# A float32 decoder trunk on one core: feature-major products as three matmuls of 256 columns, and new starts for the weight parts in their buffers

## The chip, the cores and the metric

The kernel runs on one core of one Trainium2 chip. The metric is the device time of one execution in microseconds. What follows "before" is the kernel as it was; "after" is the changed one.

## The reference

The reference is a decoder trunk of two layers over 256 tokens with 2048 features, in float32. Each layer normalises, mixes tokens, adds the result to `x`, normalises again, and adds a gated feed-forward part.

```python
for i in range(DEPTH):                       # DEPTH = 2, x is (1, 256, 2048) float32
    h = rms_norm(x, attn_norm[i])
    y = moba_attention(...) if i == 0 else mla_attention(...)
    x = x + y
    h = rms_norm(x, ffn_norm[i])
    x = x + conv_glu_ffn(h, w_gate, w_up, conv_w, conv_b, w_down)

def conv_glu_ffn(h, w_gate, w_up, conv_w, conv_b, w_down):     # 2048 -> 5632 -> 2048
    g = causal_depthwise_conv(h @ w_gate, conv_w, width=3) + conv_b
    return (silu(g) * (h @ w_up)) @ w_down
```

With 256 tokens and blocks of 256 keys, the first layer's block-sparse attention is plain causal attention with 16 heads of 128. The second is latent attention: queries and keys/values go through ranks of 512, with 128 plain and 64 rotary features a head. Nearly all the work is in the products with the weights, some 390 MB of float32, each used once.

## The kernel before

**Two parts of each number.** To keep float32 accuracy the kernel writes every operand as a high part in `float32r`, TensorE's faster float32 form, and a low part, the rest. A product is then high x high + high x low + low x high. An activation tile holds both parts side by side: columns 0 to 255 are the high part of 256 tokens, 256 to 511 the low part. This is so for `h` (the normalised input), `oT` (attention's output) and `a` (the feed-forward's inner activations).

**The stream of weights.** `Stream` carries the weights from memory to TensorE in the order of their use. A unit is one transfer of mostly 1 MB, issued by SyncE into one of three `raw` buffers (line 75). It holds four pieces of 128 x 512. For each piece, ScalarE casts the high part into a buffer `whi` (line 103) and VectorE subtracts it from the weights into `wlo` (line 104). Each of these has five buffers of 512 + 64 elements, and a piece may begin a few elements into its buffer: the function `starts` gives that for each unit and piece. There are 370 units and 1480 pieces.

**Quanta and side work.** The program is written in order by hand. A quantum is TensorE's work on one piece. Beside each quantum stand functions (`at`, `first`) that record the rest at that place: norms, evacuations, attention's steps. The final loop splits up to four pieces ahead, then records the quantum, then its side work.

**Token-major products** (`tok_major`, lines 246 to 248) load 128 tokens of the activation as weights and move a weight piece of 512 columns past them: three matmuls for each half of the tokens. They are the first attention's queries, keys and values (units 0 to 47, four head groups) and the latent layer's up-projections (units 200 to 221).

**Feature-major products** load 128 x 128 of the weight piece and move the activation. There are two forms. `feat_major` (lines 272 and 274) takes, for each of a piece's four blocks, one matmul of 512 columns (the weights' high part against both parts of the activation) and one of 256 (the weights' low part against the high part). Its result is in two halves of a PSUM bank, which `halves` adds: ScalarE copies one half to SBUF (line 293) and VectorE adds (line 297 and, with a residual, 295). Gate and up, down, and the latent layer's `wq_a` use it. `feat_half` (lines 286 to 288) takes three matmuls of 256 columns, all into the same half of a bank, so that nothing is left to add; two outputs share a bank. The output projections (`plan_wo`) and the very last down tile use it.

**Order of stages.** First attention (units 0 to 47), its output projection (48 to 63), gate and up (64 to 151), down (152 to 195), `wq_a` (196 to 199), latent attention (200 to 221), its output projection (222 to 237), gate and up (238 to 325), down (326 to 369). Attention's last heads are still under way while an output projection begins. A norm's column sums (line 361) and the spreading of its result over rows (line 371) are small matmuls between the first quanta of the stage that follows.

**Starts before.** The weight parts of gate, up, down and `wq_a` begin at 0. The others go through steps of 8 elements (32 bytes): `HEAD_STARTS` has one step for each of the twelve groups of four units, the output projections go through steps 0 to 7, two units each, and `LATENT_STARTS` has a step for each unit.

Of the kernel before, what the change touches and what calls it, by code (L numbers as in the profile page):

```python
# [10 lines left out]
F32 = mybir.dt.float32  # L11
# [6 lines left out]
P = 128  # L18
# [25 lines left out]
AHEAD_PIECES = 4  # L44
WO_OPEN = 8

UP_ORDER = ("pairs", "pairs")
DOWN_ORDER = ("pairs", "pairs")

ROOM = 64  # L50

HEAD_STARTS = (2, 1, 3, 2, 1, 3, 4, 5, 6, 7, 0, 2)
LATENT_STARTS = (1, 2, 3, 4, 5, 6, 7, 2, 2, 1, 1, 3, 3)

H_START = 8

# [58 lines left out]
def trunk(ctx: ExitStack, tc: tile.TileContext, a, out):  # L115
# [38 lines left out]
    units += units_of("ffn_down1")  # L154
    def starts(u, j):

        step = 0
        if u < 48:
            step = HEAD_STARTS[u // 4]
        elif u < 64 or 222 <= u < 238:  # L160
            step = (u - 48) // 2 % 8 if u < 64 else (u - 222) // 2
        elif u == 200:
            step = 2
        elif 201 <= u < 209:
            step = u - 201
        elif 209 <= u < 222:
            step = LATENT_STARTS[u - 209]
        return 8 * step, 8 * step

    assert len(units) == 370  # L170
    ws = Stream(nc, raw_pool, part_pool, units, starts)


# [73 lines left out]
            mm(o, hi, t_lo[:, :n], start=False, stop=False)  # L247
            mm(o, lo, t_hi[:, :n], start=False, stop=kt == k_last)  # L248

    def feat_major(state, rhs, k0, k_last, t_hi, t_lo, n, order="pairs"):  # L250

        if k0 == 0:
            state["acc"] = ps_acc.tile([P, 512], F32, name="acc")
        src, o = rhs(), state["acc"]
        ks = range(n // P)
        steps = {
            "pairs": [(k, part) for k in ks for part in "hl"],  # L260
            "low first": [(k, part) for k in ks for part in "lh"],
            "grouped": [(k, part) for part in "hl" for k in ks],
        }[order]
        for i, (k, part) in enumerate(steps):
            kt = k0 + k
            flags = dict(
                start=k0 == 0 and i == 0, stop=kt == k_last and i == len(steps) - 1,
                skip_group_check=True,
            )
            c = slice(k * P, (k + 1) * P)  # L270
            if part == "h":
                mm(o, t_hi[:, c], src[:, kt, :], **flags)  # L272
            else:
                mm(o[:, :S], t_lo[:, c], src[:, kt, :S], **flags)  # L274

    def open_half(state):
        state["acc"] = ps_acc.tile([P, 512], F32, name="acc")

    def feat_half(state, rhs, k0, k_last, first, t_hi, t_lo, n, half):

        src = rhs()
        o = state["acc"][:, half * S : (half + 1) * S]
        for k in range(n // P):
            kt = k0 + k
            w_hi, w_lo = t_hi[:, k * P : (k + 1) * P], t_lo[:, k * P : (k + 1) * P]
            mm(o, w_hi, src[:, kt, :S], start=first and k == 0, stop=False, skip_group_check=True)  # L286
            mm(o, w_hi, src[:, kt, S:], start=False, stop=False, skip_group_check=True)  # L287
            mm(o, w_lo, src[:, kt, :S], start=False, stop=kt == k_last, skip_group_check=True)  # L288

    def halves(dst, acc, base=None):  # L290

        t = small.tile([P, S], F32, name="half", bufs=2)
        nc.scalar.copy(t, acc[:, S:])  # L293
        if base is not None:
            nc.vector.tensor_tensor(t, t, base, op=ALU.add)
        dst = t if dst is None else dst
        nc.vector.tensor_tensor(dst, acc[:, :S], t, op=ALU.add)  # L297
        return dst


    class Norm:
# [77 lines left out]
    def residual(state, j, half):  # L379
        nc.vector.tensor_tensor(  # L380
            xT[:, j, :], xT[:, j, :], state["acc"][:, half * S : (half + 1) * S], op=ALU.add
        )

    def residual_halves(state, j):
        halves(xT[:, j, :], state["acc"], xT[:, j, :])

    def store(j):
        nc.sync.dma_start(out[:, j, :], xT[:, j, :])
# [258 lines left out]
    def plan_wo(norm, order):  # L647

        states = {}
        seen = set()  # L650

        done = {}
        ready = []
        last = None
        for j, kq in order:
            pr = j // 2
            states.setdefault(pr, {})
            fresh = pr not in seen
            seen.add(pr)

            def work(t_hi, t_lo, n, j=j, kq=kq, pr=pr, fresh=fresh):
                if fresh:
                    open_half(states[pr])
                feat_half(states[pr], lambda: env["oT"], 4 * kq, KD - 1, fresh, t_hi, t_lo, n, j % 2)

            last = add(work)
            done[j] = done.get(j, 0) + 1
            if done[j] == 4 and done.get(j ^ 1, 0) == 4:
                for jj in (j & ~1, j | 1):
                    at(last, residual, states[pr], jj, jj % 2)  # L670
                    ready.append((last, jj))
        nxt = 0.0
        for i, (q, jj) in enumerate(ready):
            nxt = max(nxt, q + 1)
            if i < KD - 2:
                norm.plan(int(nxt), jj)
                nxt += 2.5
            else:
                at(int(nxt) - 1, norm.now, jj)
        at(last + 3, norm.sums)  # L680
        at(last + 4, norm.rows)
        return last
# [19 lines left out]
    class FTile:  # L702
# [7 lines left out]

        def evac_gate(self):
            self.g = ffn["g"][self.j % 2]
            halves(self.g[:, 2:], self.gate["acc"])
            nc.vector.tensor_tensor(self.g[:, 2:], self.g[:, 2:], self.norm.rstd_b, op=ALU.mult)

        def conv_last(self):
            self.c = ffn["pool"].tile([P, S], F32, name="c")
# [15 lines left out]
            nc.vector.tensor_tensor(self.c, self.c, self.norm.rstd_b, op=ALU.mult)  # L733

        def product(self):
            u = halves(None, self.up["acc"])
            nc.vector.tensor_tensor(self.c, self.c, u, op=ALU.mult)

        def high(self):
            nc.scalar.copy(ffn["a"][:, self.j, :S], self.c)  # L740
# [7 lines left out]
    def plan_gate_up(layer, norm):  # L748
        for j in range(NF):
            f = FTile(layer, j, norm)  # L750
            for kind, st in (("g", f.gate), ("u", f.up)):
                for kq in range(4):
                    q = add(lambda t_hi, t_lo, n, st=st, kq=kq: feat_major(
                        st, lambda: norm.h, 4 * kq, KD - 1, t_hi, t_lo, n, UP_ORDER[layer]))
                if kind == "g":
                    if j == 0:
                        at(q, open_ffn, layer)
                    at(q, f.evac_gate)
                    at(q + 1, f.conv_last)
                    at(q + 2, f.conv_rest)  # L760
                    at(q + 3, f.silu)
                    at(q + 4, f.scaled)
                else:
                    at(q, f.product)
                    at(q + 1, f.high)
                    at(q + 2, f.low)
# [2 lines left out]

    n3 = Norm(C_AN + KD, False)  # L770

    def plan_down_feat(norm, layer):
        for j in range(KD):
            st = {}
            tail = norm is None and j == KD - 1
            if tail:
                first(len(quanta), open_half, st)
            for kq in range(NF // 4):
                if tail:
                    q = add(lambda t_hi, t_lo, n, st=st, kq=kq: feat_half(  # L780
                        st, lambda: ffn["a"], 4 * kq, NF - 1, kq == 0, t_hi, t_lo, n, 0))
                else:
                    q = add(lambda t_hi, t_lo, n, st=st, kq=kq: feat_major(
                        st, lambda: ffn["a"], 4 * kq, NF - 1, t_hi, t_lo, n, DOWN_ORDER[layer]))
            if tail:
                at(q, residual, st, j, 0)
            else:
                at(q, residual_halves, st, j)
            if norm is None:
                at(q, store, j)  # L790
            elif j < KD - 1:
                norm.plan(q + 2, j)
            else:
                at(q, norm.now, j)
                at(q + 3, norm.sums)
        return q

    plan_down_feat(n3, 0)


    att2 = ExitStack()
# [84 lines left out]

    def cq_part(state, r):
        g = par[:, C_GQA + r : C_GQA + r + 1]
        src = halves(None, state["acc"])
        hi, lo = env["cqT"][:, r, :S], env["cqT"][:, r, S:]  # L890
        nc.scalar.activation(hi, src, AF.Copy, scale=g)
        nc.vector.scalar_tensor_tensor(lo, src, g, hi.bitcast(F32), op0=ALU.mult, op1=ALU.subtract)
        if r == 0:
            cq["acc"] = att_pool.tile([P, S], F32, name="cacc", bufs=1)
            nc.scalar.activation(cq["acc"], src, AF.Square)
        else:
            sq = small.tile([P, S], F32, name="nsq", bufs=3)
            nc.scalar.activation(sq, src, AF.Square)
            nc.vector.tensor_tensor(cq["acc"], cq["acc"], sq, op=ALU.add)
# [17 lines left out]
    for r in range(4):  # L917
        state = {}
        for kq in range(4):
            q = add(lambda t_hi, t_lo, n, st=state, kq=kq: feat_major(  # L920
                st, lambda: n3.h, 4 * kq, KD - 1, t_hi, t_lo, n))
            if r == 0 and kq == 0:
                at(q, open_mla)
        at(q, cq_part, state, r)
# [97 lines left out]
    plan_wo(n4, WO_ORDER2)  # L1022
    plan_gate_up(1, n4)

    plan_down_feat(None, 1)


    assert len(quanta) == len(ws.pieces), (len(quanta), len(ws.pieces))
# [121 lines left out]
```

## Time and profile before

| | |
|---|---|
| median of 3 runs | 2138.59 us (2138.43 to 2138.74) |
| the profiled execution's own time | 2138.94 us |
| its span | 2137.1 us |
| granted TensorE clock | 1.0 |
| PE busy | 2129.4 us (100%), 12439 matmuls |
| weight loads (PEld) | 1883.5 us (88%) |
| VectorE busy | 1461.7 us (68%) |
| ScalarE busy | 1184.6 us (55%) |
| read from memory | 387.01 MB, 182 GB/s over the span |

PE is TensorE's matmuls, PEld its weight loads, DVE VectorE, ACT ScalarE, POOL GpSimd and SP SyncE. L272 is line 272 of the kernel. A row of instructions reads: engine, operation, result <- operands, shapes, number; then, by the view, durations and the first and last start, or busy time, mean duration and idle time before. Matmuls overlap in the pipeline and their ends are modelled, so that durations of one line add up to more than the span. Numbers of a stretch from a table of windows read: from:to and length, then for each engine busy time and number of instructions, then the granted clock, the DMA's busy share and GB/s.

### The profile page before, as it was taken

The page shows a single profiled execution, that of the slowest core. Times are in us where ns is not written, and L with a number is a line of the kernel's source. Part 1 is how long each engine was busy: PE and PEld are TensorE (multiplying, and loading weights), DVE is VectorE, ACT ScalarE, POOL GpSimd, SP SyncE. Part 2 cuts the span into 40 slices and gives each one's busy share as a digit, 9 for nine tenths or more (in the row PEclk, how much of TensorE's full clock was granted, in tenths as well). Part 3 has the DMA queues.
Part 4 walks back from the last instruction along what each step waited for, and adds up shares of the span by engine and source line. Part 5 has one row for each costly group of instructions (what it writes and reads, how often), then busy time and mean ns, then how long its engine had stood idle before and what let it go on. Part 6 is the DMA issues. An engine that isn't in the chain of part 4 may idle for free.

```text
span 2137.1 us, 33882 instructions
## 1 busy us (share of the span) xinstructions
PE 2129.4 (100%) x12439; PEld 1883.5 (88%) x12439; DVE 1461.7 (68%) x3246; ACT 1184.6 (55%) x2418; POOL 45.6 (2%) x37
## 2 busy tenths in 40 slices
PE   9999999999999999999999999999999999999999
PEld 7888889988888888888889889998888888888888
DVE  6766666777777777755556786777777777765554
ACT  6555555555555555545455675555555555554443
POOL 0000000000000000000000110000000000000000
PEclk9999999999999999999999999999999999999999
DMA  7444445455555555555554433555555555555553
GB/s 268 160 175 178 158 158 191 176 186 197 184 191 196 182 194 192 187 195 185 198 188 156 177 132 119 178 178 197 182 193 194 182 196 189 186 202 205 189 203 129
DMA packets 59350, 391.30 MB, mean 183 GB/s; under 512 B 6960, under 2 KB 10032, under 8 KB 13232
## 3 DMA queue, kind: packets, MB, share of 16 engines
q1 hardware_dynamic: 59040, 389.10, 51.6%
q8 instruction: 98, 1.61, 0.3%
q14 instruction: 68, 0.56, 0.1%
q10 hardware_dynamic: 144, 0.04, 0.0%
HBM read 387.01 MB, written 2.10 MB: 182 GB/s over the span
## 4 chain that ended last, share of the span: by engine, by line
PE 97%; DVE 1%; DMA 0%; issue 0%; ACT 0%; POOL 0%; SPq 0%; POOLq 0%; ACTq 0%; DVEq 0%
PE acc L272 45%; PE acc L274 24%; PE acc L247 5%; PE acc L248 5%; PE acc L246 5%; PE acc L286 3%; PE acc L288 3%; PE acc L287 3%; PE sc L511 1%; PE tp L487 1%; PE sc L558 1%; PE tp L547 0%; PE sc L514 0%; DVE wlo L104 0%; PE sc L559 0%; DMA xT<-in_xT 0%
## 5 line engine op out<-in xcount | busy, mean ns | idle before, releaser
L104 DVE TENSOR_TENSOR wlo<-raw,whi 128x512 fp32r<-128x512 f32 (+1 forms) x1480 | 991.1, 683 | 385.9 <-ACT whi L103 382.5
L103 ACT CAST whi<-raw 128x512 fp32r<-128x512 f32 (+1 forms) x1480 | 866.4, 614 | 280.3 <-PE acc L272 173.9
L272 PE MATMUL acc<-h,whi 128*128 128x512 f32 x2880 | 999.2, 390 | 0.0
L274 PE MATMUL acc<-h,wlo 128*128 128x256 f32 x2880 | 812.1, 282 | 0.0
L272 PEld LDWEIGHTS acc<-h,whi 128*128 128x128 f32 x2880 | 540.6, 188 | 113.1
L274 PEld LDWEIGHTS acc<-h,wlo 128*128 128x128 f32 x2880 | 544.3, 189 | 0.0
L272 PE MATMUL acc<-a,whi 128*128 128x512 f32 x1364 | 472.9, 390 | 0.0
L274 PE MATMUL acc<-a,wlo 128*128 128x256 f32 x1364 | 384.6, 282 | 0.0
L272 PEld LDWEIGHTS acc<-a,whi 128*128 128x128 f32 x1364 | 256.0, 188 | 53.7
L274 PEld LDWEIGHTS acc<-a,wlo 128*128 128x128 f32 x1364 | 257.8, 189 | 0.0
L293 ACT COPY half<-acc 128x256 f32<-128x256 f32 x211 | 78.7, 373 | 308.3 <-PE acc L274 308.1
L246 PE MATMUL acc<-whi,h 128*128 128x512 f32 (+1 forms) x448 | 177.1, 395 | 0.0
L247 PE MATMUL acc<-wlo,h 128*128 128x512 f32 (+1 forms) x448 | 171.0, 382 | 0.5 <-DVE wlo L104 0.5
L248 PE MATMUL acc<-whi,h 128*128 128x512 f32 (+1 forms) x448 | 170.1, 380 | 0.0
L286 PE MATMUL acc<-oT,whi 128*128 128x256 f32 x512 | 146.9, 287 | 0.0
L288 PE MATMUL acc<-oT,wlo 128*128 128x256 f32 x512 | 143.8, 281 | 0.0
L287 PE MATMUL acc<-oT,whi 128*128 128x256 f32 x512 | 143.7, 281 | 0.0
L297 DVE TENSOR_TENSOR g<-acc,half 128x256 f32<-128x256 f32 x88 | 37.4, 425 | 121.1 <-ACT half L293 121.1
L247 PEld LDWEIGHTS acc<-wlo,h 128*128 128x128 f32 x448 | 84.4, 188 | 17.2 <-DVE wlo L104 2.1
L248 PEld LDWEIGHTS acc<-whi,h 128*128 128x128 f32 x448 | 84.3, 188 | 16.8
L246 PEld LDWEIGHTS acc<-whi,h 128*128 128x128 f32 x448 | 84.4, 188 | 15.7 <-ACT whi L103 1.2
L286 PEld LDWEIGHTS acc<-oT,whi 128*128 128x128 f32 x512 | 96.7, 189 | 0.2
(153 smaller groups left out, 1594.1 us busy)
## 6 DMA issues: line engine op xcount, KB each, us to landing
raw<-in_ffn_gu SPq DMA_DIRECT2D x176, 1024.0 KB, 4.8
raw<-in_ffn_down SPq DMA_DIRECT2D x88, 1024.0 KB, 4.8
raw<-in_moba_wk SPq DMA_DIRECT2D x16, 1024.0 KB, 4.8
raw<-in_moba_wv SPq DMA_DIRECT2D x16, 1024.0 KB, 4.8
raw<-in_moba_wo SPq DMA_DIRECT2D x16, 1024.0 KB, 4.8
raw<-in_mla_wo SPq DMA_DIRECT2D x16, 1024.0 KB, 4.8
raw<-in_moba_wq SPq DMA_DIRECT2D x13, 1024.0 KB, 4.8
raw<-in_mla_wkv_a SPq DMA_DIRECT2D x8, 576.0 KB, 3.8
```

The costliest lines, as they stand in the source:

```text
L103: self.nc.scalar.copy(hi[:, :n], w)
L104: self.nc.vector.tensor_tensor(lo[:, :n], w, hi[:, :n].bitcast(F32), op=ALU.subtract)
L246: mm(o, hi, t_hi[:, :n], start=kt == 0, stop=False)
L247: mm(o, hi, t_lo[:, :n], start=False, stop=False)
L248: mm(o, lo, t_hi[:, :n], start=False, stop=kt == k_last)
L272: mm(o, t_hi[:, c], src[:, kt, :], **flags)
L274: mm(o[:, :S], t_lo[:, c], src[:, kt, :S], **flags)
L286: mm(o, w_hi, src[:, kt, :S], start=first and k == 0, stop=False, skip_group_check=True)
L287: mm(o, w_hi, src[:, kt, S:], start=False, stop=False, skip_group_check=True)
L288: mm(o, w_lo, src[:, kt, :S], start=False, stop=kt == k_last, skip_group_check=True)
L293: nc.scalar.copy(t, acc[:, S:])
L297: nc.vector.tensor_tensor(dst, acc[:, :S], t, op=ALU.add)
```

## The change

- `feat_major` is now the three-matmul form (the old `feat_half`, under the old name) and all feature-major products use it; the two-matmul form is gone. For each 128 x 128 block of the weights it issues high x high, high x low and low x high, 256 columns each, into one half of a bank.
- With it go `halves` and `residual_halves`: ScalarE's copy and VectorE's adding of the halves. Gate, up, `wq_a` and the residual read the one half of the bank directly.
- `starts` has three values in place of the lists: 8 elements (32 bytes) for token-major units, 24 elements (96 bytes) for feature-major ones, and 20 elements (80 bytes) for 39 single pieces, each the first of a unit in the set `entries`. These lie in the output projections, just behind the first quanta of gate/up and `wq_a`, at the start of down, and then every eighth unit of gate and up and every eleventh of down.

```diff
-UP_ORDER = ("pairs", "pairs")
-DOWN_ORDER = ("pairs", "pairs")
-HEAD_STARTS = (2, 1, 3, 2, 1, 3, 4, 5, 6, 7, 0, 2)
-LATENT_STARTS = (1, 2, 3, 4, 5, 6, 7, 2, 2, 1, 1, 3, 3)
+BY_TOKEN, BY_FEATURE, ENTRY = 8, 24, 20
...
     def starts(u, j):
-        step = 0
-        if u < 48:
-            step = HEAD_STARTS[u // 4]
-        elif u < 64 or 222 <= u < 238:
-            step = (u - 48) // 2 % 8 if u < 64 else (u - 222) // 2
-        elif u == 200:
-            step = 2
-        elif 201 <= u < 209:
-            step = u - 201
-        elif 209 <= u < 222:
-            step = LATENT_STARTS[u - 209]
-        return 8 * step, 8 * step
+        if u < 48 or 200 <= u < 222:
+            return BY_TOKEN, BY_TOKEN
+        b = ENTRY if j == 0 and u in entries else BY_FEATURE
+        return b, b
+
+    entries = {52, 56, 60, 197, 224, 226, 228, 230, 234}
+    for first_unit, n, every in ((65, 87, 8), (152, 44, 11), (239, 87, 8), (326, 44, 11)):
+        entries |= set(range(first_unit, first_unit + n, every))
...
-    def feat_major(state, rhs, k0, k_last, t_hi, t_lo, n, order="pairs"):
-        if k0 == 0:
-            state["acc"] = ps_acc.tile([P, 512], F32, name="acc")
-        src, o = rhs(), state["acc"]
...
-            if part == "h":
-                mm(o, t_hi[:, c], src[:, kt, :], **flags)
-            else:
-                mm(o[:, :S], t_lo[:, c], src[:, kt, :S], **flags)
...
-    def feat_half(state, rhs, k0, k_last, first, t_hi, t_lo, n, half):
+    def feat_major(state, rhs, k0, k_last, first, t_hi, t_lo, n, half=0):
+        if first and half == 0 and "acc" not in state:
+            open_bank(state)
         src = rhs()
         o = state["acc"][:, half * S : (half + 1) * S]
         for k in range(n // P):
             kt = k0 + k
             w_hi, w_lo = t_hi[:, k * P : (k + 1) * P], t_lo[:, k * P : (k + 1) * P]
             mm(o, w_hi, src[:, kt, :S], start=first and k == 0, stop=False, skip_group_check=True)
             mm(o, w_hi, src[:, kt, S:], start=False, stop=False, skip_group_check=True)
             mm(o, w_lo, src[:, kt, :S], start=False, stop=kt == k_last, skip_group_check=True)
-    def halves(dst, acc, base=None):
-        t = small.tile([P, S], F32, name="half", bufs=2)
-        nc.scalar.copy(t, acc[:, S:])
-        if base is not None:
-            nc.vector.tensor_tensor(t, t, base, op=ALU.add)
-        dst = t if dst is None else dst
-        nc.vector.tensor_tensor(dst, acc[:, :S], t, op=ALU.add)
-        return dst
...
         def evac_gate(self):
             self.g = ffn["g"][self.j % 2]
-            halves(self.g[:, 2:], self.gate["acc"])
-            nc.vector.tensor_tensor(self.g[:, 2:], self.g[:, 2:], self.norm.rstd_b, op=ALU.mult)
+            nc.vector.tensor_tensor(
+                self.g[:, 2:], self.gate["acc"][:, :S], self.norm.rstd_b, op=ALU.mult
+            )
...
         def product(self):
-            u = halves(None, self.up["acc"])
-            nc.vector.tensor_tensor(self.c, self.c, u, op=ALU.mult)
+            nc.vector.tensor_tensor(self.c, self.c, self.up["acc"][:, :S], op=ALU.mult)
...
     def cq_part(state, r):
         g = par[:, C_GQA + r : C_GQA + r + 1]
-        src = halves(None, state["acc"])
+        src = state["acc"][:, :S]
```

More of the change, by code (lines that the diff above doesn't have):

```diff
@@ L248, in tok_major, with open_bank @@
             mm(o, lo, t_hi[:, :n], start=False, stop=kt == k_last)
-    def feat_major(state, rhs, k0, k_last, t_hi, t_lo, n, order="pairs"):
-        if k0 == 0:
-            state["acc"] = ps_acc.tile([P, 512], F32, name="acc")
-        src, o = rhs(), state["acc"]
[L258 to L270, printed above, removed]
-            if part == "h":
-                mm(o, t_hi[:, c], src[:, kt, :], **flags)
-            else:
-                mm(o[:, :S], t_lo[:, c], src[:, kt, :S], **flags)
-    def open_half(state):
+    def open_bank(state):
         state["acc"] = ps_acc.tile([P, 512], F32, name="acc")
-    def feat_half(state, rhs, k0, k_last, first, t_hi, t_lo, n, half):
+    def feat_major(state, rhs, k0, k_last, first, t_hi, t_lo, n, half=0):
+        if first and half == 0 and "acc" not in state:
+            open_bank(state)
         src = rhs()
@@ L382, in residual @@
         )
-    def residual_halves(state, j):
-        halves(xT[:, j, :], state["acc"], xT[:, j, :])
     def store(j):
@@ L662, in work @@
                 if fresh:
-                    open_half(states[pr])
-                feat_half(states[pr], lambda: env["oT"], 4 * kq, KD - 1, fresh, t_hi, t_lo, n, j % 2)
+                    open_bank(states[pr])
+                feat_major(states[pr], lambda: env["oT"], 4 * kq, KD - 1, fresh, t_hi, t_lo, n, j % 2)
             last = add(work)
@@ L753, in plan_gate_up @@
                     q = add(lambda t_hi, t_lo, n, st=st, kq=kq: feat_major(
-                        st, lambda: norm.h, 4 * kq, KD - 1, t_hi, t_lo, n, UP_ORDER[layer]))
+                        st, lambda: norm.h, 4 * kq, KD - 1, kq == 0, t_hi, t_lo, n))
                 if kind == "g":
@@ L770, in trunk, with plan_down_feat @@
     n3 = Norm(C_AN + KD, False)
-    def plan_down_feat(norm, layer):
+    def plan_down_feat(norm):
         for j in range(KD):
             st = {}
-            tail = norm is None and j == KD - 1
-            if tail:
-                first(len(quanta), open_half, st)
             for kq in range(NF // 4):
[L779 to L788, printed above, removed]
+                q = add(lambda t_hi, t_lo, n, st=st, kq=kq: feat_major(
+                    st, lambda: ffn["a"], 4 * kq, NF - 1, kq == 0, t_hi, t_lo, n))
+            at(q, residual, st, j, 0)
             if norm is None:
@@ L796, in plan_down_feat @@
         return q
-    plan_down_feat(n3, 0)
+    plan_down_feat(n3)
     att2 = ExitStack()
@@ L920, in trunk @@
             q = add(lambda t_hi, t_lo, n, st=state, kq=kq: feat_major(
-                st, lambda: n3.h, 4 * kq, KD - 1, t_hi, t_lo, n))
+                st, lambda: n3.h, 4 * kq, KD - 1, kq == 0, t_hi, t_lo, n))
             if r == 0 and kq == 0:
@@ L1023, in trunk @@
     plan_gate_up(1, n4)
-    plan_down_feat(None, 1)
+    plan_down_feat(None)
     assert len(quanta) == len(ws.pieces), (len(quanta), len(ws.pieces))
```

## The prediction

> **What bounds the kernel now.** I read the page first, then the waits of PE, then the instructions of one line in chosen windows, and last the timeline, since only starts show how fast TensorE really goes. The page:
>
> ```profile
> span 2137.1 us, 33882 instructions
> ...
> PE 2129.4 (100%) x12439; PEld 1883.5 (88%) x12439; DVE 1461.7 (68%) x3246; ACT 1184.6 (55%) x2418; POOL 45.6 (2%) x37
> ...
> PE 97%; DVE 1%; DMA 0%; issue 0%; ACT 0%; POOL 0%; SPq 0%; POOLq 0%; ACTq 0%; DVEq 0%
> PE acc L272 45%; PE acc L274 24%; PE acc L247 5%; PE acc L248 5%; PE acc L246 5%; PE acc L286 3%; PE acc L288 3%; PE acc L287 3%; PE sc L511 1%; PE tp L487 1%; PE sc L558 1%; PE tp L547 0%; PE sc L514 0%; DVE wlo L104 0%; PE sc L559 0%; DMA xT<-in_xT 0%
> ...
> L104 DVE TENSOR_TENSOR wlo<-raw,whi 128x512 fp32r<-128x512 f32 (+1 forms) x1480 | 991.1, 683 | 385.9 <-ACT whi L103 382.5
> L103 ACT CAST whi<-raw 128x512 fp32r<-128x512 f32 (+1 forms) x1480 | 866.4, 614 | 280.3 <-PE acc L272 173.9
> L272 PE MATMUL acc<-h,whi 128*128 128x512 f32 x2880 | 999.2, 390 | 0.0
> L272 PE MATMUL acc<-a,whi 128*128 128x512 f32 x1364 | 472.9, 390 | 0.0
> L293 ACT COPY half<-acc 128x256 f32<-128x256 f32 x211 | 78.7, 373 | 308.3 <-PE acc L274 308.1
> ```
>
> The waits of PE, longest first; this is the first row:
>
> ```profile
> PE acc L247 <- DVE wlo L104: 1.2, 3, 0.8
> ```
>
> TensorE is the whole chain and waits for nobody worth naming. So the time is the sum of the steps from one matmul's start to the next, and an edit counts only by what it does to that step. The mean durations (390, and 282 at L274) do not tell the step, because matmuls overlap: 4244 of each would be 2852 us. The step comes from first and last starts, here of L272 in a window of gate/up and one of the down product:
>
> ```profile
> L272 PE MATMUL acc<-h,whi x1155: 390/390/390, 419.9 to 819.9; 128*128 128x512 f32 x193
> L272 PE MATMUL acc<-a,whi x578: 390/390/390, 899.6 to 1099.7; 128*128 128x512 f32 x193
> ```
>
> 400.0 us over 1154 steps is 346.6 ns, 200.1 over 577 is 346.8: every pair of a 512- and a 256-column matmul takes 346.7 ns, whichever operand moves. There are 2880 + 1364 = 4244 pairs, 1471 us, 69% of the span as the chain also says. The profiled execution took 2138.94 us (span 2137.1 and 1.8 around it); the median of three is 2138.59, so sums against the one hold for the other.
>
> **The main edit: the pair becomes three matmuls of 256.** The columns stay 768, so only overhead can move. The kernel before has such triples already: in the output projections, L286 to L288, with the weight parts at eight different starts in their buffers, and in the last down tile. First counts, in order: second projection at 96 bytes, first projection at 96 bytes, second at 128, first at 160, and the last down tile at 0:
>
> ```profile
> L286 PE MATMUL acc<-oT,whi x32: 276/276/279, 1343.5 to 1354.0; 128*128 128x256 f32 x32
> L286 PE MATMUL acc<-oT,whi x32: 281/281/282, 342.4 to 353.3; 128*128 128x256 f32 x32
> L286 PE MATMUL acc<-oT,whi x32: 282/283/285, 1354.4 to 1365.5; 128*128 128x256 f32 x32
> L286 PE MATMUL acc<-oT,whi x32: 285/285/285, 364.9 to 376.1; 128*128 128x256 f32 x32
> L286 PE MATMUL acc<-a,whi x44: 277/279/280, 2117.8 to 2132.9; 128*128 128x256 f32 x44
> ```
>
> Then the first and last of three of these from the timeline, which has the hundredths:
>
> ```profile
> 1343.50 0.28 PE L286 MATMUL acc<-oT,whi 128*128 128x256 f32 x1
> ...
> 1354.04 0.28 PE L286 MATMUL acc<-oT,whi 128*128 128x256 f32 x1
> ...
> 342.36 0.28 PE L286 MATMUL acc<-oT,whi 128*128 128x256 f32 x1
> ...
> 353.32 0.28 PE L286 MATMUL acc<-oT,whi 128*128 128x256 f32 x1
> ...
> 2117.83 0.28 PE L286 MATMUL acc<-a,whi 128*128 128x256 f32 x1
> ...
> 2132.88 0.28 PE L286 MATMUL acc<-a,whi 128*128 128x256 f32 x1
> ```
>
> A triple therefore takes 10.54/31 = 340.0 ns in the second projection at 96 bytes, 10.96/31 = 353.5 ns in the first at the same 96 bytes, 15.05/43 = 350.0 ns in the last tile at 0, and about 360 (11.1/31 and 11.2/31) in the two others. Within each stretch the step repeats to the nanosecond through five buffers, both halves of a bank and all values of k. These are locked patterns: weight load and moving operand stay in one phase to each other. The start sets which patterns are open; since 96 bytes shows two, something else picks between them. I call them the 340 and the 353.5 lock.
>
> In the 340 lock 4244 triples save 4244 x (346.7 - 340.0) = 28.3 us; in the 353.5 lock they cost 4244 x 6.8 = 28.9 us. This is the whole question. Two things can have picked: the phase at entry (the stretches before differ), or the moving operand's address. In the built programs `h` and the second `oT` lie 160 bytes past a multiple of 1024, `a` and the first `oT` 672. Gate/up and `wq_a` move `h`, which is on the side of the 340 row. For the address speaks nothing else: the pairs run at the same 346.7 on `h` and on `a`. For the phase speaks that the two were entered differently: the 353.5 stretch follows another one without a break, the 340 one a stretch still cut by attention's matmuls. The single pieces at 80 bytes put a different step into the phase just where it is disturbed: one norm's column sums show such a disturbance,
>
> ```profile
> 1404.17 0.28 PE L274 MATMUL acc<-h,wlo 128*128 128x256 f32 x1
> 1404.29 0.50 PE L361 MATMUL tp<-ones,nacc 128*128 128x1 f32 x4
> 1404.65 0.48 PE L272 MATMUL acc<-h,whi 128*128 128x512 f32 x1
> ```
>
> with 0.32 us then to the next start. No row has a piece at 80 bytes, so whether it leads into the 340 lock is my guess, not a reading; I take the 340 row, the one with gate/up's address class, and keep 353.5 as the other end.
>
> A rule speaks against this reading. The Trainium skill, "TensorE: Matmul & The Clock Gate", Part 2 (step 1 of what each phase is for), says that weights have a read port of their own and that loading them takes nothing from the running matmul; and its "Wait — 56ns, not 53.3ns?" gives a step of columns / 2.4 plus about 2.5 ns for each matmul. By it no start matters, a triple would be 327.5 ns against the pair's 325.0, and the sum would be 2138.9 + 4244 x 2.5 ns = 2149.5 us. The trace disagrees on the starts (340 to 360 ns for identical work) and on the sizes.
>
> **The other edits.** The output projections go to the same lock. Two windows of them, after attention is through:
>
> ```profile
> 322.40:399.20 76.80, 76.80 (x650) 76.80 (x649) 50.79 (x96) 42.58 (x82) 0.00 (x0) 1.00 0.53 189
> 1343.50:1400.10 56.60, 56.60 (x482) 56.60 (x481) 41.15 (x82) 33.93 (x68) 0.00 (x0) 1.00 0.53 187
> ```
>
> They hold 216 and 160 triples (54 and 40 pieces of four). At 340 these take 73.4 and 54.4, a gain of 3.4 and 2.2; at 353.5 they gain 0.4 and 0. The 136 triples among attention's matmuls can gain at most 13.5 ns each, 1.8; I take 0.9. The last tile's 44 gain 10 ns each, 0.4.
>
> Token-major products now all start at 32 bytes. Undisturbed stretches at 32, 64, 96 and 160 bytes, one start in three matmuls of 512:
>
> ```profile
> L246 PE MATMUL acc<-whi,h x28: 389/389/395, 29.3 to 47.7; 128*128 128x512 f32 x28
> L246 PE MATMUL acc<-whi,h x23: 393/394/397, 13.2 to 28.6; 128*128 128x512 f32 x23
> L246 PE MATMUL acc<-whi,h x18: 394/394/398, 127.7 to 139.4; 128*128 128x512 f32 x18
> L246 PE MATMUL acc<-whi,h x18: 392/395/398, 179.6 to 191.5; 128*128 128x512 f32 x18
> ```
>
> Steps 681, 700, 688 and 700 ns. Of the first attention's twelve groups of 32 triples, two have 32 bytes already, two have 96 (64 x 7 = 0.4 us) and eight other starts, taken at 700 like the two shown (256 x 19 = 4.9); the latent part adds under 1. The gain is 0 to 6; I take 4.5, since interruptions cut these stretches short.
>
> The 39 pieces at 80 bytes are 156 triples at 340 to 360: 0 to 3.1 us, taken as 1.0.
>
> The removed copies (L293, 211 of 373 ns) and the adds behind them sit on ACT and DVE and save nothing: a piece takes TensorE 4 x 346.7 = 1387 ns, ACT's and DVE's part of it 614 and 683. At 340 it is 1360, twice the slower of them, so weights still come in time; if that cover went, DVE's 683 would be the bound only below half the present step. The evacuation gets shorter by one engine's turn, no wait is added, no DMA moves, and nothing is queued behind anything new. There are 4244 more matmuls with a weight load each; the projections show that rate, three loads in 340 ns, without a stall.
>
> **Sum.** 28.3 + 3.4 + 2.2 + 0.9 + 0.4 + 4.5 - 1.0 = 38.7 us; 2138.9 - 38.7 = **2100.2 us**. Its own range is 2096 (all of the token gain, free 80-byte pieces) to 2108 (a few stretches of 128 triples lost at 1.7 us each).
>
> **Rivals.**
> *The 353.5 lock.* After a disturbance the stream settles at 353.5 and the 80-byte pieces don't bring it out. For: the first projection's row. Against: the second's, with `h`'s address. 4244 + 44 + 216 + 160 = 4664 triples lose 13.5 each, 63.0, and the 0.9 of the opening: 2164 us. It decides from 38.7/13.5 = 2867 triples on, 61% of them. Chance 0.16.
> *Address decides.* `a` and the first `oT` lock at 353.5, `h` at 340: 1364 + 44 + 216 triples x 13.5 = 21.9: 2122 us. Chance 0.10.
> *Lost and found.* The 340 lock holds only part of the way between 80-byte pieces; with half, 2100.2 + 31.5 = 2132 us; 2108 to 2134 in all. Chance 0.08; what lands within 0.2% of before has 0.02.
> *A price for each matmul.* Splitting costs what the last tile shows, 350.0, whatever the start: 4664 x 10 = 46.6, and 0.9: 2148 us, slower. Against it the 340 row. This is how the fixed part of the step in that page of the Trainium skill would act, at the trace's size. Chance 0.06.
> *It doesn't do what it says.* In the built program every feature-major product is three of 256 columns at 96 or 80 bytes, so this has no share.
>
> **Numbers.** The 340 lock all through has what is left, 0.58. Faster by over 0.2% (about what a measurement of this kernel tells from no change): 0.58 + 0.10 + 0.08 = 0.76; within it 0.02; slower 0.16 + 0.06 = 0.22. The range 2095 to 2148 leaves out the 353.5 lock, 0.16, and a little at its ends. The likeliest, 2100, is the forecast.
>
> **What would show it.** Right: the gate/up triples' first and last starts 340 ns apart per triple, durations near 276, PE still the whole chain, ACT's copies gone without a trace in the span, token-major triples at 681. Wrong: 350 to 360 ns in gate/up; a difference between `h` and `a` (address); steps that change at an 80-byte piece or after a norm's matmuls (phase lost or found); PE waiting for `wlo`.

## The result and the profile after

The changed kernel takes 2129.27 us, the median of five executions from 2128.61 to 2130.11, against 2138.74 for the kernel before, measured beside it. The ratio is 0.9956 with a 95% interval of 0.9941 to 0.9970: faster by 9.5 us, a quarter of the 38.7 that were forecast. The page of the profiled execution, which took 2129.42 us:

```profile
span 2127.6 us, 42062 instructions
...
PE 2119.6 (100%) x16683; PEld 2045.3 (96%) x16683; DVE 1388.7 (65%) x3035; ACT 1140.9 (54%) x2207; POOL 45.6 (2%) x37
...
PE 98%; DVE 1%; issue 0%; ACT 0%; POOL 0%; DMA 0%; SPq 0%; POOLq 0%; ACTq 0%
PE acc L256 26%; PE acc L255 26%; PE acc L257 26%; PE acc L239 5%; PE acc L238 5%; PE acc L240 5%; PE sc L467 1%; PE tp L443 1%; PE sc L514 1%; PE tp L503 0%; PE sc L470 0%; PE sc L515 0%; DVE wlo L100 0%; DVE junk L373 0%; POOL hr L386 0%
...
L255 PE MATMUL acc<-h,whi 128*128 128x256 f32 x2880 | 802.7, 279 | 0.0
```

TensorE is still the whole chain; the copies and adds that went took 73 us from DVE and 44 from ACT, and no stage below shows a gain that needs them. L255 to L257 are the three matmuls of a triple. Their mean duration of 279 ns hides what matters: it is the mean of two values. First and last starts in gate/up of the first and of the second layer, and in down of the first and of the second:

```profile
L255 PE MATMUL acc<-h,whi x123: 276/276/277, 444.4 to 485.8; 128*128 128x256 f32 x123
L255 PE MATMUL acc<-h,whi x123: 281/281/282, 1384.8 to 1427.9; 128*128 128x256 f32 x123
L255 PE MATMUL acc<-a,whi x172: 276/276/277, 874.3 to 932.5; 128*128 128x256 f32 x172
L255 PE MATMUL acc<-a,whi x172: 281/281/282, 1876.4 to 1936.8; 128*128 128x256 f32 x172
```

The first layer takes 41.4/122 = 339 and 58.2/171 = 340 ns a triple, the second 43.1/122 = 353.3 and 60.4/171 = 353.2. The two layers' feed-forward parts are the same code. At 96 bytes the duration is a quick sign: 276 belongs to the 340 lock, 281 to 353.3. The same four stretches as windows, of the kernel before:

```profile
399.28:888.20 488.92, 488.92 (x2824) 1.00 0.54 189
888.20:1132.25 244.05, 244.05 (x1410) 1.00 0.54 191
1400.12:1889.03 488.91, 488.91 (x2824) 1.00 0.54 189
1889.03:2133.11 244.08, 244.08 (x1453) 1.00 0.53 186
```

and of the changed one:

```profile
392.77:872.90 480.13, 480.13 (x4232) 1.00 0.54 194
872.90:1112.47 239.57, 239.57 (x2114) 1.00 0.55 194
1376.79:1874.96 498.17, 498.17 (x4232) 1.00 0.52 187
1874.96:2123.60 248.64, 248.64 (x2113) 1.00 0.52 182
```

All stages, from the first weight matmul of each to that of the next (the last one to the last matmul's start):

| stage | before, us | after, us | difference |
|---|---|---|---|
| first attention | 298.46 | 294.88 | -3.6 |
| its output projection | 95.81 | 92.14 | -3.7 |
| gate/up, layer 0 | 488.92 | 480.13 | -8.8 |
| down, layer 0 | 244.05 | 239.57 | -4.5 |
| wq_a | 22.65 | 22.27 | -0.4 |
| latent attention | 137.34 | 136.85 | -0.5 |
| its output projection | 107.88 | 105.20 | -2.7 |
| gate/up, layer 1 | 488.91 | 498.17 | +9.3 |
| down, layer 1 | 244.08 | 248.65 | +4.6 |

Before rounding the differences add up to -10.2; the first weight matmul starts 0.7 us later than before (5.75 us into the span in place of 5.02), which leaves 9.5. Up to the second layer's gate/up the forecast holds stage by stage; from there on the sign turns.

### The profile page after: what moved, and what is told of

The parts are those of the page before. It is cut to its first block, busy times and chain, and to the rows that moved or that the text cites. A ratio compares the mean times of both kernels' runs of the same rounds, so it can differ in the third digit from the quotient of the medians.

```text
span 2127.6 us, 42062 instructions
## 1 busy us (share of the span) xinstructions
PE 2119.6 (100%) x16683; PEld 2045.3 (96%) x16683; DVE 1388.7 (65%) x3035; ACT 1140.9 (54%) x2207; POOL 45.6 (2%) x37
## 4 chain that ended last, share of the span: by engine, by line
PE 98%; DVE 1%; issue 0%; ACT 0%; POOL 0%; DMA 0%; SPq 0%; POOLq 0%; ACTq 0%
PE acc L256 26%; PE acc L255 26%; PE acc L257 26%; PE acc L239 5%; PE acc L238 5%; PE acc L240 5%; PE sc L467 1%; PE tp L443 1%; PE sc L514 1%; PE tp L503 0%; PE sc L470 0%; PE sc L515 0%; DVE wlo L100 0%; DVE junk L373 0%; POOL hr L386 0%
## 5 line engine op out<-in xcount | busy, mean ns | idle before, releaser
L99 ACT CAST whi<-raw 128x512 fp32r<-128x512 f32 (+1 forms) x1480 | 878.7, 614 | 477.8 <-PE acc L256 328.0
L255 PE MATMUL acc<-h,whi 128*128 128x256 f32 x2880 | 802.7, 279 | 0.0
L256 PE MATMUL acc<-h,whi 128*128 128x256 f32 x2880 | 802.3, 279 | 0.0
L257 PE MATMUL acc<-h,wlo 128*128 128x256 f32 x2880 | 802.1, 279 | 0.0
L255 PEld LDWEIGHTS acc<-h,whi 128*128 128x128 f32 x2880 | 546.5, 190 | 0.0
L257 PEld LDWEIGHTS acc<-h,wlo 128*128 128x128 f32 x2880 | 540.8, 188 | 0.0
L256 PEld LDWEIGHTS acc<-h,whi 128*128 128x128 f32 x2880 | 540.7, 188 | 0.0
L256 PE MATMUL acc<-a,whi 128*128 128x256 f32 x1408 | 392.3, 279 | 0.0
L255 PE MATMUL acc<-a,whi 128*128 128x256 f32 x1408 | 392.3, 279 | 0.0
L257 PE MATMUL acc<-a,wlo 128*128 128x256 f32 x1408 | 392.2, 279 | 0.0
L255 PEld LDWEIGHTS acc<-a,whi 128*128 128x128 f32 x1408 | 267.3, 190 | 0.0
L257 PEld LDWEIGHTS acc<-a,wlo 128*128 128x128 f32 x1408 | 264.4, 188 | 0.0
L256 PEld LDWEIGHTS acc<-a,whi 128*128 128x128 f32 x1408 | 264.3, 188 | 0.0
L255 PE MATMUL acc<-oT,whi 128*128 128x256 f32 x512 | 145.0, 283 | 0.0
L257 PE MATMUL acc<-oT,wlo 128*128 128x256 f32 x512 | 141.7, 277 | 0.0
L669 DVE TENSOR_TENSOR g<-acc,rstd_b 128x256 f32<-128x256 f32 x88 | 37.4, 425 | 131.0 <-PE acc L257 128.1
L676 ACT ACTIVATE c<-g,par 128x256 f32<-128x256 f32 x88 | 53.1, 603 | 110.2 <-DVE g L669 110.2
```

The costliest lines, as they stand in the source:

```text
L99: self.nc.scalar.copy(hi[:, :n], w)
L669: nc.vector.tensor_tensor(self.g[:, 2:], self.gate["acc"][:, :S], self.norm.rstd_b, op=ALU.mult)
L676: nc.scalar.activation(self.c, self.g[:, 2:], AF.Identity, bias=par[:, cb : cb + 1], scale=self.cw(2))
```

## The experiments

Two theories. *Phase*: which lock the stream is in is settled when it restarts behind a disturbance, here a norm's small matmuls, and holds until something shifts it; the 80-byte pieces don't. *Layer*: something of the second layer allows only 353.3 there. Times of the kernel before, run beside these, were 2138.9 to 2139.0 in the median.

**Fourteen starts for the single pieces.**

```diff
-        b = ENTRY if j == 0 and u in entries else BY_FEATURE
+        b = singles.get(u, BY_FEATURE) if j == 0 else BY_FEATURE
+    tried = (0, 4, 8, 12, 16, 28, 32, 36, 40, 44, 48, 52, 56, 60)
+    singles = {u: ENTRY for u in entries}
+    singles |= dict(zip((*range(73, 152, 8), 152, 163, 174, 185), tried))
+    singles |= dict(zip((*range(247, 326, 8), 326, 337, 348, 359), tried))
```

> The changed kernel, but the 28 single pieces of gate/up and down that stand away from a norm (every eighth unit of gate/up, every eleventh of down) each get another start: 0, 16, 32, 48, 64, 112, 128, 144, 160, 176, 192, 208, 224, 240 bytes in this order, the same list in both layers. The pieces behind the norms keep 80. Phase theory (a lock is a phase; a single piece of the right start shifts it, 80 bytes carries either lock through): the second layer starts at 353.5 ns a triple and drops to 340 behind one of the fourteen, and the first layer leaves 340 behind at least one. If that happens in the middle of the second layer the time is about 2115 us. Layer theory (something of the second layer, an address or a neighbour, allows only 353.5 there): all fourteen pass and the second layer stays at 353.5 to its end, 2129 us or more. Guess: phase 0.7.

One execution, 2110.73 us. Here the second layer came out of its norm in the 340 lock, so it wasn't a test of the way out at the first piece, but it tested two others. Single pieces at 32 and at 208 bytes led from 340 to 353.3, in both layers; the pieces that came after those, at 48 and at 224, led back to 340, in both layers. The ten others kept 340. The second layer's gate/up before the piece at 32, behind it, and behind the one at 48:

```profile
L259 PE MATMUL acc<-h,whi x120: 276/276/276, 1477.4 to 1517.8; 128*128 128x256 f32 x120
L259 PE MATMUL acc<-h,whi x123: 281/281/281, 1519.6 to 1562.7; 128*128 128x256 f32 x123
L259 PE MATMUL acc<-h,whi x124: 276/276/279, 1564.8 to 1606.7; 128*128 128x256 f32 x124
```

One piece of 1.4 us sets the step of the 40 us behind it. The layer theory falls: the second layer runs at 340 too, with `h` and with `a`.

**No single pieces.**

```diff
-        b = ENTRY if j == 0 and u in entries else BY_FEATURE
+        b = BY_FEATURE
```

> The changed kernel with every feature-major piece at 96 bytes, none at 80. If 80-byte pieces are what leads into the 340 lock, gate/up and down of the first layer go to 353.5 too: 2129.3 + 2112 x 13.3 ns = about 2157 us. If they only carry through what there is, the first layer stays at 340 without them and the 39 x 4 triples at 353 are saved where the lock is 340: about 2 us less, 2127 us; the second layer may fall either way, since its first piece behind the norm is now another: with 340 there too about 2099 us.

2100.43, 2100.09, 2128.00 and 2100.04 us; the ratio of the four has an interval of 0.9792 to 0.9911. In the profiled execution (2100.43) both layers stand at 340 from end to end:

```profile
L255 PE MATMUL acc<-h,whi x1387: 276/276/276, 400.8 to 872.1; 128*128 128x256 f32 x199
L255 PE MATMUL acc<-h,whi x1387: 276/276/276, 1383.8 to 1855.1; 128*128 128x256 f32 x199
```

So the 340 lock doesn't need the 80-byte pieces. The one at 2128.00 stands 27.9 us above: one layer's 2112 triples x 13.3 ns are 28.2. It has no trace, so that it is one layer is inferred from its time.

**All at 0 bytes: the split alone.**

```diff
-BY_TOKEN, BY_FEATURE, ENTRY = 8, 24, 20
+BY_TOKEN, BY_FEATURE, ENTRY = 8, 0, 0
```

> The changed kernel with all feature-major pieces at 0 bytes: the split into three alone, with the token-major starts. By the last tile's 350.0 ns a triple against the pair's 346.7: 4244 x 3.3 = 14.1 us more for the former pairs, less 3.6 us of token-major gain in the first attention, the output projections 376 x 5 = 2 us less: 2138.7 + 14.1 - 5.6 = about 2147 us. If the split itself is free and the gain is all from it, about 2129 us.

2154.84 us, ratio 1.0074 (1.0057 to 1.0091): slower, and by more than the 2147 expected, since 0 bytes has two locks as well. Gate/up of the first layer, of the second, and down of the second:

```profile
L255 PE MATMUL acc<-h,whi x1315: 277/278/281, 419.9 to 879.8; 128*128 128x256 f32 x188
L255 PE MATMUL acc<-h,whi x1303: 281/281/281, 1419.9 to 1879.9; 128*128 128x256 f32 x187
L255 PE MATMUL acc<-a,whi x704: 281/281/281, 1901.1 to 2149.5; 128*128 128x256 f32 x176
```

350.0, 353.3 and 353.3 ns: the second layer's 2112 triples at 3.3 more are the 7 us between 2147 and 2154. The split at 0 bytes costs, even with the gain of the token-major starts in the sum; at 96 bytes, in the 340 lock, it gains.

**Pairs and triples at sixteen starts.** The kernel before, with gate/up of the first layer as pairs and of the second as triples.

```diff
+        for base in (64, 238):
+            if base <= u < base + 80:
+                return 4 * ((u - base) // 5), 4 * ((u - base) // 5)
         return 8 * step, 8 * step
```

> The kernel before with a sweep in place of the start at 0: in gate/up of the first layer, still as pairs of 512 and 256 columns, the start goes through 0, 16, 32, ... 240 bytes, five units (80 pairs) each; in gate/up of the second layer, as triples of 256, the same. It shows what each start allows. Phase theory: triples at 96 bytes lock at 340 or at 353.5 and no start lies below 340; pairs are at 346.7 at 0, and if the overhead is a conflict of weight load and moving operand, pairs have a start with 340 as well. If pairs stay at 346.7 for all starts, the gain of the change needs the split.

One execution, 2152.6 us. Steps in ns from the trace, over 70 of the 80 groups at each start (the first pairs, at 0, lie beside the norm, and stand from elsewhere in the kernel; the first triples too, here the two values that 0 bytes showed):

| start, bytes | 0 | 16 | 32 | 48 | 64 | 80 | 96 | 112 | 128 | 144 | 160 | 176 | 192 | 208 | 224 | 240 |
|---|---|---|---|---|---|---|---|---|---|---|---|---|---|---|---|---|
| pair | 346.7 | 353.3 | 346.7 | 346.7 | 346.7 | 346.7 | 353.3 | 353.3 | 346.7 | 353.3 | 351.1 | 349.3 | 350.0 | 349.3 | 353.4 | 350.0 |
| triple | 350 or 353.3 | 352.0 | 360.0 | 354.9 | 355.0 | 353.3 | 340.0 | 356.3 | 352.0 | 360.0 | 356.0 | 355.0 | 360.0 | 354.3 | 353.3 | 350.0 |

Pairs at 32 and at 96 bytes, then triples at 32 and at 96:

```profile
L275 PE MATMUL acc<-h,whi x80: 392/394/395, 456.0 to 483.3; 128*128 128x512 f32 x80
L275 PE MATMUL acc<-h,whi x80: 389/397/398, 566.9 to 594.8; 128*128 128x512 f32 x80
L289 PE MATMUL acc<-h,whi x79: 280/283/283, 1461.5 to 1489.6; 128*128 128x256 f32 x79
L289 PE MATMUL acc<-h,whi x80: 276/276/277, 1575.0 to 1601.9; 128*128 128x256 f32 x80
```

Here no start takes a pair below 346.7, at 96 bytes it is worse, and only the triple at 96 reaches 340: by these rows the gain needs both edits at once. But the run is one execution, and a stretch shows one pattern of its start, not all: triples at 224 bytes, 353.3 here, run at 340 in the last experiment below. That pairs have no better pattern is therefore not shown. The Trainium skill, "TensorE: Matmul & The Clock Gate", Part 2 (what each phase is for), has a read port for weights that takes nothing from a running matmul. In these rows the same three matmuls take 340 to 360 ns at sixteen starts of their weights, so where the weights lie does change the step here; whether a port has to do with it, no run shows.

**The changed kernel again, twelve executions.**

> The changed kernel as it is, again, to see whether the lock of a layer is the same in every execution. The last experiment with nothing at 80 bytes had one execution of four at 2128.0 against 2100.0, which is one layer's 2112 triples at 353.3 in place of 340 (28.2 us). If the lock behind a norm is chance, the times stand at about 2101, 2129 and 2157 (none, one, both layers at 353.3), with nothing between; if the 80-byte piece behind the second norm always ends in the same lock, all stand at 2129.

Ten from 2128.70 to 2130.43, and two at 2101.74 and 2102.19; nothing between and none near 2157. With the first five it makes 15 of 17 at 2129. So the lock behind a norm varies from one execution to the next, with a strong lean. The profiled one again has 340 in the first layer and 353.3 in the second; in the others it can't be told which layer it is.

The 80-byte pieces are not cleared by this. The changed kernel's trace shows the second layer's gate/up entering in the 340 lock; behind twelve triples come the norm's column sums, and behind four more the spreading of its result over rows (L330). The next L255 is the first of the 80-byte piece, with nothing at 96 bytes between. A row of L255, then three of the timeline:

```profile
L255 PE MATMUL acc<-h,whi x12: 276/276/276, 1376.8 to 1380.5; 128*128 128x256 f32 x12
1382.58 0.28 PE L257 MATMUL acc<-h,wlo 128*128 128x256 f32 x1
1382.79 0.43 PE L330 MATMUL tp<-ident,rstd 128*128 128x128 f32 x2
1382.97 0.36 PE L255 MATMUL acc<-h,whi 128*128 128x256 f32 x1
```

So the stream restarts on that piece. With it 15 of 17 executions stand where one lost layer puts them, without it 1 of 4. The piece may make 353.3 likelier there; four executions, on another chip than the twelve, are too few to show it, and no run settles it.

**One piece at 48 bytes.**

```diff
-        b = ENTRY if j == 0 and u in entries else BY_FEATURE
+        b = 12 if j == 0 and u == 247 else ENTRY if j == 0 and u in entries else BY_FEATURE
```

> The changed kernel with one of 1200 feature-major pieces changed: the single piece at unit 247, the second of the second layer's gate/up, starts at 48 bytes in place of 80. Phase theory (a 48-byte piece leads out of the 353.3 lock, as it did twice in the experiment with fourteen starts, and 80 bytes carries either lock through): where the second layer starts at 353.3 it goes to 340 from unit 247 on, 1984 triples x 13.3 = 26.4 us less: 2129.3 - 26.4 = 2102.9 us. Rival (the second layer's lock comes from somewhere else, or what followed in that experiment hung on the other starts): 2129 us, a single piece moves nothing.

2102.44, 2103.71, 2103.70 and 2103.96 us; ratio 0.9834 (0.9822 to 0.9847). None of four at 2129, where the same kernel without this edit had 15 of 17. Three stand 1.4 us above the other, about what eight units at 353.3 cost before the way out at unit 247 (128 triples x 13.3 = 1.7). In the profiled execution, 2102.44, the second layer had come out of its norm at 340 by itself, so the three are read by their times alone.

**All single pieces at 48 bytes.**

```diff
-BY_TOKEN, BY_FEATURE, ENTRY = 8, 24, 20
+BY_TOKEN, BY_FEATURE, ENTRY = 8, 24, 12
```

> The changed kernel with all 39 single pieces at 48 bytes in place of 80. If 48 bytes leads to 340 from either lock, both layers run at 340 in every execution; the 156 triples cost up to 356 - 340 each, 2.5 us: about 2102 us, no run at 2129. If from the 340 lock it leads out (not tried yet), the lock alternates from one single piece to the next, and the time is about 2129.

2102.30 to 2107.26, median 2104.49 us; why one execution stands at 2107.26 is open, since it has no trace. The traced one, 2104.39, has the way out itself, between units 239 and 247 and behind the piece at 247:

```profile
L255 PE MATMUL acc<-h,whi x124: 280/281/281, 1384.7 to 1428.1; 128*128 128x256 f32 x124
L255 PE MATMUL acc<-h,whi x124: 276/276/279, 1429.9 to 1471.7; 128*128 128x256 f32 x124
```

43.4/123 = 352.8 ns in the first, 41.8/123 = 339.8 in the second. Behind all later single pieces it stays at 340.

**Pieces at 48 bytes behind the norms only.**

```diff
-    entries = {52, 56, 60, 197, 224, 226, 228, 230, 234}
-    for first_unit, n, every in ((65, 87, 8), (152, 44, 11), (239, 87, 8), (326, 44, 11)):
-        entries |= set(range(first_unit, first_unit + n, every))
+    entries = {52, 65, 66, 67, 197, 198, 228, 239, 240, 241}        # with ENTRY = 12
```

> The changed kernel with 48-byte single pieces only at the first of units 52, 65 to 67, 197, 198, 228 and 239 to 241, all others at 96 bytes. If 48 bytes leads to 340 from either lock and nothing disturbs the stream later: 2100 us in every execution, the version that beats both. If the lock is lost elsewhere, executions at 2100 and 2128 side by side as in the one without single pieces.

2100.67 to 2102.26, median 2101.14 us. In its trace the stream restarted on the piece at 239 and stood at 353.3 behind it, the piece at 240 did not lead out, and the one at 241 did; the rows follow each of the three:

```profile
L253 PE MATMUL acc<-h,whi x12: 281/281/281, 1384.8 to 1388.7; 128*128 128x256 f32 x12
L253 PE MATMUL acc<-h,whi x11: 281/281/281, 1390.9 to 1394.4; 128*128 128x256 f32 x11
L253 PE MATMUL acc<-h,whi x1356: 276/276/287, 1396.2 to 1856.9; 128*128 128x256 f32 x194
```

So 48 bytes is no sure way out. That it hangs on the phase which the piece meets would fit, but isn't shown. From 340 it led away in no trace.

**Without the second norm's small matmuls.**

```diff
-        at(last + 3, norm.sums)
-        at(last + 4, norm.rows)
+        if norm is n2:
+            at(last + 3, norm.sums)
+            at(last + 4, norm.rows)
+        else:
+            at(last + 4, lambda: setattr(norm, "rstd_b", n2.rstd_b))
```

> The changed kernel without the column sums and the spreading of rows (six small matmuls) behind the second layer's output projection: the second feed-forward part uses the first one's row scales instead, so this leaves out a part of the computation. Everything else, the 80-byte pieces too, is as in the changed kernel. If those small matmuls are what throws the stream out of the 340 lock, the lock that the output projection ends with goes on: both layers at 340 in every execution, 2129.3 - 28.2 - about 1 = 2100 us. If the 80-byte piece itself, or something else of the second layer, picks 353.3, the time stays at 2128 us.

2128.45 to 2128.92 us in five executions: the expected time is missed, and by itself it would speak against the phase theory. The trace says otherwise. Gate/up of the first layer and of the second:

```profile
L255 PE MATMUL acc<-h,whi x121: 281/281/281, 400.4 to 442.8; 128*128 128x256 f32 x121
L255 PE MATMUL acc<-h,whi x124: 276/276/276, 1411.0 to 1452.8; 128*128 128x256 f32 x124
```

The second layer, no longer disturbed, went on at 340 as expected, through its 80-byte pieces, the one at 239 too. The first, whose norm is still there, fell to 353.3, and its 80-byte pieces did not bring it out. So the layers have changed places, and the layer with the disturbance is the one that lost. Only one of the five is traced.

**Pieces at 224 bytes behind the norms.** As the one with 48, with `ENTRY = 56`.

> The last version with 48-byte pieces behind the norms, with 224 bytes in place of 48 there. With fourteen starts, 224 led from 353.3 to 340 in both layers, and the steady pattern at 224 is itself 353.3. If it is surer than 48 (which failed at two of three pieces behind the second norm in the profiled execution) all executions stand at 2100 us, up to 1.7 us below; if it fails three times in a row somewhere, single executions stand at 2128.

2099.13 to 2100.75, median 2100.42 us; ratio 0.9819 (0.9805 to 0.9832). The second layer stood at 353.3 behind the piece at 239, on which the stream restarted, and the piece at 240 took it out. Behind 239, behind 240, and from 241 on:

```profile
L253 PE MATMUL acc<-h,whi x12: 280/281/281, 1383.2 to 1387.1; 128*128 128x256 f32 x12
L253 PE MATMUL acc<-h,whi x12: 276/276/277, 1388.9 to 1392.6; 128*128 128x256 f32 x12
L253 PE MATMUL acc<-h,whi x1351: 276/276/276, 1396.0 to 1855.0; 128*128 128x256 f32 x193
```

With the two among the fourteen starts this is three of three that met 353.3 and led out of it. In the first layer the pieces at 224 bytes ran at 340 themselves and cost nothing. This version beats both kernels: 38.6 us under the kernel before, 28.9 under the changed one.

## Why the prediction was right or wrong

The failed step is the one that the text called a guess: that the single pieces at 80 bytes lead into the 340 lock. They did not lead out of 353.3. In the traces of the changed kernel they carried 340 through the first layer and 353.3 through the second, as each had settled behind its norm, and the first of them, on which the stream restarts there, may have helped it to the wrong lock. Two patterns had been read at 96 bytes, one stretch each, and the text gave the more favourable one 0.58, leaning on an address class that turned out not to matter.

What came is the mechanism of the rival "the 353.5 lock" (the stream settles there behind a disturbance, and the 80-byte pieces don't bring it out), in one layer of two. "Lost and found", priced at 2132 us for half of the way, lies near the measured 2129.27, but it had the lock come and go between the pieces; that its number is close is luck. No rival had one layer lost as a whole.

By terms. The pairs: 28.3 us forecast in all; the first layer's gate/up, down and `wq_a` gave 13.7, nearly its half (2176 triples x 6.67 = 14.5, with the 80-byte pieces not yet taken off); the second layer lost 13.8 in place of gaining 13.8 and the last tile's 0.4. That term alone is the miss: 28 of the 29 us. The output projections: 6.5 forecast with the triples among attention's matmuls, 6.4 measured. Token-major: 4.5 forecast, 4.1 measured (3.6 and 0.5), at the step that was read, here (287.7 - 268.6)/28 = 682 ns in the first attention:

```profile
L238 PE MATMUL acc<-whi,h x29: 389/389/390, 268.6 to 287.7; 128*128 128x512 f32 x29
```

The 80-byte pieces: each triple takes 353 where the stream is at 340, within the 340 to 360 given, so all 156 cost 2.0 us with both layers at 340; 1.0 was taken. The lower end of the sum's own range, 2096, is set low: the token gain of 6 and free pieces that it names give 2100.2 - 1.5 - 1.0 = 2097.7. Copies and adds at nothing: right.

The rivals. *Address decides* fell: `a` ran at 340 in the first layer and `h` at 353.3 in the second. *A price for each matmul* was right for the split (350 to 353.3 at 0 bytes, slower by 0.7%) but not with the start. *The 353.5 lock* everywhere never came: no execution of the changed kernel stands near 2157, where both layers at 353.3 would put it. And the all-340 sum was right as a sum: 2100.2 forecast, 2101.7 and 2102.2 in the two executions of the changed kernel that stand 27 us below the others, and 2100.0 to 2100.4 in the three without single pieces that kept the lock.

What stays open: why the restart leans to 353.3 behind one norm and to 340 behind the other, and why the first layer was the one at 353.3 in the one trace without the second norm's matmuls. The code ahead of the first layer's gate/up is the same there. No run here shows what it hangs on, nor that a lock is a phase of weight load and moving operand; that stays my reading of the repeating steps.

## What to carry to other kernels

Where TensorE is the whole chain, read its step from first and last starts over a stretch and compare stretches of the same form: one average over a line hid two values 4% apart. When a trace shows two steps for the same work, the chance of each stays unknown until several executions have been timed and something has been seen to lead out of the worse one. Every execution of a set is worth a look: two clusters 27 us apart told more than their median.

## What was not expected of the hardware

In a dense stream of matmuls with a weight load each, TensorE's step locks to a pattern that repeats to the nanosecond, and for one and the same instructions there can be two patterns (340.0 and 353.3 ns for three of 256 columns), kept for hundreds of microseconds across buffers, banks and operands. The step goes with the start of the weights in SBUF, in steps of 16 bytes: 340 to 360 ns for a triple, 346.7 to 353.4 for a pair, each as one execution showed it. A single piece of 1.4 us at another start can move the stream from one to the other, in both directions.
